# Two hybrid decoder layers on one core: S5 matmuls in a hand-written order, its U and y reordered through DRAM, layer 1's S5 operands made during layer 0's feed forward

## The chip, the core and the metric

One core of a Trainium2 chip runs the whole kernel in one launch: TensorE (matmul), VectorE, ScalarE, GpSimd, and SyncE, which issues most DMAs. The metric is the device time of one execution in microseconds, as a median of runs.

## The reference, cut to what matters

512 tokens, width 1024, two layers, all in float32. Each layer projects the tokens and mixes them in three branches, merges these with sigmoid gates, then an output projection, a layer norm, a feed forward of width 4096 and a second layer norm.

```python
u_pool, u_ssm, q, kv, g_nsa, g_merge = split(x @ w_in)
y_pool = pool_mixer(u_pool, ...)            # trailing means, grouped 128x128 matmul
# S5: 32 groups of 16 channels, 64 complex states each
h[t] = a * h[t-1] + Bbar @ u[t]             # associative scan over the 512 tokens
y = Re(C @ h) + d * u ; z = gelu(y) ; y_ssm = z * sigmoid(z @ w_glu + b_glu)
y_nsa = compressed / selected / window attention, gated
x = layer_norm(ALPHA * x + merged @ w_out)
x = layer_norm(ALPHA * x + relu(x @ w_ff1)**2 @ w_ff2)
```

In the compressed branch, keys and values of 32-token blocks pass through a two-layer MLP (`gelu(flat @ w1) @ w2`) before the attention.

## The kernel before, in words

Every large product is float32 as three fp32r matmuls (high x high, high x low, low x high), `mm3_`, lines 93 to 102. It is a generator: one step is three matmuls. Weights come through `wload` (line 70): SyncE loads 512 KB into one of two staging buffers `wst`, ScalarE casts it to `wh`, VectorE or GpSimd makes the rest `wl`, four buffers of each. `proj` is one 128-channel projection, 8 steps.

A planner orders each engine's instructions by priority and estimated time, except where `manual_schedule` keeps the written order. TensorE's order is written by hand in the attention part, where `run` takes a pattern string: a letter is a step of a named generator, a dot a step of `fill` (GLU, merge of the S5 branch, gates).

`s5_branch` (line 470) works in four rounds r of 8 groups. A round makes operands on GpSimd from the parameters (`step` and `cmul`, lines 450 to 455: Z, W, and the powers E by doubling), which ScalarE spreads into block form (525, 528). TensorE makes K (535) and transposes Z to lq (545), multiplies lq with U (551, the "q" product); VectorE and GpSimd rotate by E, scan along the chunks and rotate back into the state S (554 to 572); TensorE adds K x U and W x S into py (575, 577); a gelu follows. U (128 partitions, 4 tokens per chunk side by side) is made from the projection by 16 small ScalarE copies a round (465), and y is turned back by 16 more (582). In layer 0 rounds 2 and 3 take their E from VectorE; in layer 1 all of it is on GpSimd.

In a layer the branches are called one after the other: pooling (four projections, each followed by its 128x128 product), S5, the merge of the pooling branch, `nsa_early` (values, gate, two key projections); the planner interleaves them. Then follows `nsa_branch`: query projections, the compressed branch (lines 710 to 720: 32 float32 matmuls a layer with 65 columns, each recorded twice; its weights w in two buffers), and the attention.

`feed_forward` runs 8 chunks of up and down. In layer 0 its last chunk is woven with the next layer's U projection (`norm_xw`), then GpSimd applies the layer norm's gain and bias (`ln_affine`), and the residual goes to DRAM (`xd`, line 1148).

Of the kernel before, what the change touches and what calls it, by code (L numbers as in the profile page):

```python
# [9 lines left out]
F32 = mybir.dt.float32  # L10
R = mybir.dt.float32r
# [15 lines left out]
class Kern:  # L27
# [41 lines left out]
    def wload(self, ap, pool=None):  # L69

        n = ap.shape[1]
        with ExitStack() as order:
# [6 lines left out]
            self.nc.sync.dma_start(st, ap)  # L79
# [135 lines left out]
    def ln_affine(self, rs, g, b):  # L215

        gl = self.nc.gpsimd
        with self.tc.manual_schedule(engines={mybir.EngineType.Pool}):
            for r in (rs[3], rs[0], rs[1], rs[2]):
                for h in range(2):  # L220
                    s = slice(h * 512, (h + 1) * 512)
                    gl.tensor_tensor(r[:, s], r[:, s], g[:, s], OP.mult)  # L222
                    gl.tensor_tensor(r[:, s], r[:, s], b[:, s], OP.add)
# [81 lines left out]
    def pool_branch(self, i, pb):  # L305
        nc = self.nc
        nxt = self.proj(i, 4)
        wh, wl = self.wload(self.A["wpool"][i])
        for g in range(4):
            ps = nxt  # L310
            w = 2 << g
            u, *a = [self.t(pb, [128, 528], F32, "e", 6) for k in range(2 if g == 0 else 3)]
            for q in (u, *a):
                nc.vector.memset(q[:, 0:16], 0.0)
            nc.scalar.copy(u[:, 16:], ps)
            s, d = u, 1
            while d < w:
                nc.vector.tensor_tensor(a[0][:, 16:], s[:, 16:], s[:, 16 - d:528 - d], OP.add)
                s, a, d = a[0], a[::-1], 2 * d
            nc.vector.tensor_tensor(s[:, 16:32], s[:, 16:32], self.pfix[:, g, :], OP.mult)  # L320
            zf = s[:, 16:]
            nc.vector.scalar_tensor_tensor(zf, zf, 1.0 / w, u[:, 16:], op0=OP.mult, op1=OP.subtract)
            zh = self.t(pb, [128, 512], R, "e", 6)
            zl = self.t(pb, [128, 512], R, "e", 6)
            self.hi_lo(zh, zl, zf)
            if g < 3:
                nxt = self.proj(i, 5 + g)
            p2 = self.psum("o")
            c = slice(g * 128, (g + 1) * 128)
            self.mm3(p2, [((wh[:, c], wl[:, c]), (zh, zl))])  # L330
# [4 lines left out]
            self.y_pool.append((yh, yl))  # L335

# [119 lines left out]

    def s5_inputs(self, pss):

        self.U = []
        for pu in pss:  # L460
            u = self.t(self.hp, [128, 512], R, "hi_b").bitcast(F32).rearrange("p (g c) -> p g c", g=4)
            for g in range(4):
# [6 lines left out]
    def s5_branch(self, i):  # L469
        nc, v, tc = self.nc, self.nc.vector, self.tc  # L470
        gl = nc.gpsimd
        are, aim, are2, aim2, kre, kim, dec = self.s5a
        pr, pi = self.s5ph
        zt = []
        with tc.tile_pool(name=f"s5{i}", bufs=1, reuse_waits="tile") as sp:
            T = lambda shape, dt, tag, bufs=1: self.t(sp, shape, dt, tag, bufs)
            U = self.U
            for r in range(4):
                u = U[r]
                gs = slice(i * 16 + 4 * r, i * 16 + 4 * r + 4)  # L480
                col = lambda q, n: q[:, gs].unsqueeze(1).unsqueeze(3).to_broadcast([128, 2, 4, n])
                dd = T([32, 4, 32], F32, "dd")
                nc.sync.dma_start(dd, self.A["ddiag"][i, :, 4 * r:4 * r + 4])
                bc = T([128, 4, 64], F32, "bc", 2)
                nc.sync.dma_start(bc, self.A["s5bc"][i, :, :, r * 64:(r + 1) * 64])

                Zc = T([128, 2, 4, 64], F32, "Zc")
                Wc = T([128, 2, 4, 80], F32, "Wc")

                def step(y, x, ar, ai):  # L490
                    n = x.shape[3]
# [755 lines left out]
```

## Time and profile before

| | |
|---|---|
| median of 3 runs | 1804.28 us (1802.28 to 1805.58) |
| the profiled execution | 1810.14 us |
| its span, first to last instruction | 1808.4 us |
| TensorE busy in it | 1694.7 us, 94% |
| mean granted TensorE clock | 0.976 of 2.4 GHz |
| VectorE, ScalarE, GpSimd busy | 1142.7, 795.7, 514.2 us |
| DMA | 161.67 MB, 89 GB/s over the span |

The profile is of one execution; times in it are microseconds from its first instruction. An engine's busy time includes what an instruction waits inside; "idle" is time between its instructions, and the profile names what released the next one. A granted clock between 0.5 and 1 is the mean of a stretch at 1.2 and at 2.4 GHz.

### The profile page before, as it was taken

What the parts mean: (1) busy time and instruction counts of PE and PEld (TensorE: products, weight loads), DVE (VectorE), ACT (ScalarE), POOL (GpSimd) and SP (SyncE); (2) the same over time, 40 slices, a digit from 0 to 9 for tenths busy, and PEclk for the clock granted to TensorE, in tenths of its full rate; (3) what the DMA queues carried; (4) which work ended last, traced back from release to release, by engine and by line L of the source; (5) the groups of instructions that cost most, each with busy time, mean ns of one, the idle gap of its engine ahead of it and who ended that gap; (6) DMA issues with size and microseconds to landing.
All of it is one profiled execution on the core that took longest, in us unless ns stands there. A gap on an engine that the chain in (4) does not pass through costs nothing.

```text
span 1808.4 us, 22625 instructions
## 1 busy us (share of the span) xinstructions
PE 1694.7 (94%) x8356; PEld 1409.7 (78%) x8356; DVE 1142.7 (63%) x2161; ACT 795.7 (44%) x1517; POOL 514.2 (28%) x612
## 2 busy tenths in 40 slices
PE   3989889999999999999998889999999999999996
PEld 2877777778779888888896777777787888888885
DVE  8786667776578645444566555776766684444447
ACT  2645545656534333223264456465564342223321
POOL 3966421321023202000059995122212060000002
PEclk9999999999999999999999999899999999999998
DMA  5221151111251334232222212311124233222231
GB/s 189 76 82 44 43 172 49 57 59 59 82 176 38 121 104 145 94 104 95 76 78 83 83 53 69 128 59 57 61 61 141 91 105 105 93 94 93 94 103 61
DMA packets 51375, 161.67 MB, mean 89 GB/s; under 512 B 10816, under 2 KB 11584, under 8 KB 51264
## 3 DMA queue, kind: packets, MB, share of 16 engines
q1 hardware_dynamic: 48960, 154.85, 25.9%
q10 hardware_dynamic: 2304, 5.37, 0.9%
q8 instruction: 65, 1.06, 0.2%
q14 instruction: 46, 0.38, 0.1%
HBM read 153.92 MB, written 6.29 MB: 89 GB/s over the span
## 4 chain that ended last, share of the span: by engine, by line
PE 65%; DVE 15%; POOL 8%; ACT 6%; issue 3%; DMA 2%; ACTq 0%; SPq 0%; DVEq 0%; POOLq 0%
PE mm L98 12%; PE mm L99 12%; PE mm L100 12%; PE s L99 4%; PE s L100 4%; PE s L98 4%; PE t L100 3%; PE t L98 3%; PE t L99 3%; ACT st L582 3%; PE o L749 2%; PE t L848 2%; DVE wl L85 1%; POOL wl L85 1%; ACT wh L82 1%
## 5 line engine op out<-in xcount | busy, mean ns | idle before, releaser
L82 ACT CAST wh<-wst 128x1024 fp32r<-128x1024 f32 (+1 forms) x260 | 269.9, 1041 | 450.9 <-PE s L100 217.0
L98 PE MATMUL mm<-xh,wh 128*128 128x512 f32 (+1 forms) x1088 | 432.3, 397 | 6.1 <-ACT hi_b L465 3.1
L85 DVE TENSOR_TENSOR wl<-wst,wh 128x1024 fp32r<-128x1024 f32 (+1 forms) x202 | 269.1, 1333 | 252.1 <-ACT wh L82 251.7
L100 PE MATMUL mm<-xh,wl 128*128 128x512 f32 (+1 forms) x1088 | 423.9, 390 | 0.0
L99 PE MATMUL mm<-xl,wh 128*128 128x512 f32 (+1 forms) x1088 | 423.7, 389 | 0.0
L98 PEld LDWEIGHTS mm<-xh,wh 128*128 128x128 f32 x1088 | 208.1, 191 | 44.6 <-ACT hi_b L465 3.8
L100 PEld LDWEIGHTS mm<-xh,wl 128*128 128x128 f32 x1088 | 207.8, 191 | 42.2 <-issue 0.2
L99 PEld LDWEIGHTS mm<-xl,wh 128*128 128x128 f32 x1088 | 208.0, 191 | 35.4 <-issue 0.2
L85 POOL TENSOR_TENSOR wl<-wst,wh 128x1024 fp32r<-128x1024 f32 (+2 forms) x58 | 143.3, 2473 | 284.2 <-ACT wh L82 284.2
L222 POOL TENSOR_TENSOR xm<-xm,ln_g 128x512 f32<-128x512 f32 x24 | 43.9, 1830 | 357.4 <-PE t L238 357.4
L193 POOL TENSOR_TENSOR xm<-xm,ln_g 128x512 f32<-128x512 f32 x9 | 12.2, 1367 | 323.9 <-ACT xm L192 323.9
L821 ACT ACTIVATE P<-P,mx 128x512 f32<-128x512 f32 (+3 forms) x128 | 71.3, 559 | 69.8 <-DVE mx L819 69.2
L819 DVE CUSTOM_DVE_ANT_0 P<-s,mask 128x512 f32<-128x512 f32 (+3 forms) x128 | 59.4, 486 | 32.2 <-PE s L816 30.8
L62 DVE TENSOR_TENSOR Pl<-t,Ph 128x384 fp32r<-128x384 f32 (+1 forms) x96 | 57.2, 597 | 28.4 <-ACT Ph L61 28.4
L1034 DVE TENSOR_TENSOR xm<-xm,t 128x512 f32<-128x512 f32 x56 | 38.5, 688 | 55.3 <-PE t L100 54.5
L1034 DVE TENSOR_TENSOR xm<-xm,s 128x512 f32<-128x512 f32 x56 | 38.3, 684 | 44.0 <-PE s L100 44.0
L828 POOL TENSOR_SCALAR P<-P,sm,gate 128x128 f32<-128x128 f32 x32 | 14.5, 453 | 168.8 <-DVE sm L823 113.3
L1017 DVE TENSOR_TENSOR mt<-mt 128x512 f32<-128x512 f32 x64 | 55.9, 873 | 4.7 <-ACT mt L1016 4.7
L99 PE MATMUL mm<-lo_a,wh 128*128 128x512 f32 x128 | 52.4, 409 | 3.4 <-DVE lo_a L334 3.4
L61 ACT CAST Ph<-t 128x384 fp32r<-128x384 f32 (+1 forms) x96 | 48.4, 506 | 15.1 <-PE t L848 14.0
L98 PE MATMUL mm<-hi_a,wh 128*128 128x512 f32 x128 | 53.0, 416 | 0.2 <-ACT hi_a L333 0.2
L99 PE MATMUL s<-wl,hi_a 128*128 128x512 f32 x136 | 53.0, 390 | 0.0
(409 smaller groups left out, 3858.6 us busy)
## 6 DMA issues: line engine op xcount, KB each, us to landing
wst<-in_wf_dram SPq DMA_DIRECT2D x128, 512.0 KB, 3.5
wst<-in_win_dram SPq DMA_DIRECT2D x80, 512.0 KB, 3.2
wst<-in_wup_dram SPq DMA_DIRECT2D x24, 512.0 KB, 3.5
wst<-in_wout_dram SPq DMA_DIRECT2D x16, 512.0 KB, 4.2
xd<-xm SPq DMA_DIRECT2D x8, 512.0 KB, 4.1
w<-in_w_dram SPq DMA_DIRECT2D x8, 512.0 KB, 4.9
xm<-xd SPq DMA_DIRECT2D x8, 512.0 KB, 5.1
xm<-in_x_dram SPq DMA_DIRECT2D x4, 512.0 KB, 5.6
```

What stands on the lines that cost most here:

```text
L61: a = self.nc.scalar.copy(hi, src)
L62: b = self.nc.vector.tensor_tensor(lo, src, hi.bitcast(F32), OP.subtract)
L82: self.nc.scalar.copy(wh, st)
L85: e.tensor_tensor(wl, st, wh.bitcast(F32), OP.subtract)
L98: mm(out, ah, bh, start=first and i == 0, stop=False, **kw)
L99: mm(out, ah, bl, start=False, stop=False, **kw)
L100: mm(out, al, bh, start=False, stop=last and i == n - 1, **kw)
L582: nc.scalar.copy(dst[:, j], py[32 * j:32 * j + 32, g, :])
L819: v.tensor_tensor_reduce(out=p, in0=ss[qb], in1=self.mask[:, 384 - 128 * qb:512], scale=-1.0, scalar=3e38, op0=OP.add, op1=OP.min, accum_o ...
L821: nc.scalar.activation(p, p, AF.Exp, bias=mx[:, qb:qb + 1], scale=-1.0, accum_out=c)
L1017: v.tensor_tensor(h, h, h, OP.mult)
L1034: v.tensor_tensor(r, r, ps, OP.add)
```

## The change

- S5's TensorE order is written by hand. `first_branches` draws fill steps (pooling projections, `nsa_early`, the pooling's grouped products, its merge, in this order: 180 steps) between the pieces of the S5 generator `s5_`, which yields how many steps to put in. Round r is split in `front(r)` and `back(r)`.
- The pooling branch keeps its four results and does the grouped products after `nsa_early`.
- U and y: ScalarE copies the whole bank in one instruction, `across` writes it to DRAM and loads it back in four pieces in the other order.
- Operands Z, W and E of a round lie in one tile `zwe`, two of them. For layer 1 they are made by GpSimd alone in layer 0's feed forward (`s5_ahead`, one round per chunk from chunk 1), written to DRAM (`s5d`, 1.70 MB a round) and loaded from there by `s5_`.
- The gain and bias of layer 0's last layer norm are loaded at chunk 7, in halves, into the hidden-activation buffers; the residual's DRAM writes are issued after the first operand load of layer 1.
- Compressed branch: four weight buffers, loaded at its start; 66 columns for 65; both products before the evictions.
- The attention's pattern: the last step of the compressed softmax (the transposes of ec) stands after 15 dots, three score steps and two value steps, before after 11 dots; the product with it comes behind the first transposes.

```diff
+    def first_branches(self, i, pb):
+        def others():
+            yield from self.pool_(i, pb, res)
+            self.share = 2
+            yield from self.merge_(i, 0, self.y_pool)
+        res, n = [], 0
+        fill = others()
+        with self.tc.manual_schedule(engines={mybir.EngineType.PE}):
+            for k in self.s5_(i):
+                if i and k and self.late:
+                    for tb in range(4):
+                        self.nc.sync.dma_start(self.xd[tb], self.late[tb])
+                    self.late = None
+                for _ in range(k):
+                    n += next(fill, 1) is None
+            for _ in fill:
+                n += 1
+        return res[0]
...
+    def across(self, src):
+        d = self.t(self.dr, [4, 32, 4, 128], F32, "across", 8)
+        self.nc.sync.dma_start(d.rearrange("b x a c -> (b x) a c"), src)
+        def load(out):
+            for a in range(4):
+                self.nc.sync.dma_start(out[32 * a:32 * a + 32], d[:, :, a].rearrange("b x c -> x b c"))
+        return load
...
     def s5_inputs(self, pss):
         for pu in pss:
-            u = self.t(self.hp, [128, 512], R, "hi_b").bitcast(F32).rearrange("p (g c) -> p g c", g=4)
-            for g in range(4):
-                src = pu[32 * g:32 * g + 32].rearrange("p (c j) -> p j c", j=4)
-                for j in range(4):
-                    self.nc.scalar.copy(u[32 * j:32 * j + 32, g, :], src[:, j])
-            self.U.append(u)
+            q = self.t(self.hp, [128, 512], R, "lo_b").bitcast(F32).rearrange("p (j c) -> p j c", j=4)
+            self.nc.scalar.copy(q, pu.rearrange("p (c j) -> p j c", j=4))
+            self.U.append(self.across(q))
...
+    def s5_ahead(self, i, after):
+        with self.tc.tile_pool(name=f"s5a{i}", bufs=1, reuse_waits="tile") as pool:
+            qs = [self.t(pool, [128, 3328], F32, f"zwe{k}") for k in range(2)]
+            for r in range(5):
+                with self.tc.issue_after(after):
+                    if r < 2:
+                        self.nc.gpsimd.memset(qs[r][:, 0:2304], 0.0)
+                    if r < 4:
+                        self.s5_operands(pool, i, r, qs[r % 2], self.nc.gpsimd, True)
+                if r:
+                    with self.tc.issue_after(self.loaded):
+                        self.nc.sync.dma_start(self.s5d[r - 1], qs[(r - 1) % 2])
+                yield
...
+            def operands(r):
+                dd = T([32, 4, 32], F32, "dd")
+                nc.sync.dma_start(dd, self.A["ddiag"][i, :, 4 * r:4 * r + 4])
+                q = zwe[r % 2]
+                if i == 0:
+                    self.s5_operands(sp, i, r, q, v if r >= 2 else gl)
+                else:
+                    with tc.high_priority():
+                        nc.sync.dma_start(q, self.s5d[r])
+                return (dd, *self.s5_views(q))
...
+            def front(r):
+                dd, Z, W, EE = first if r == 0 else operands(r)
+                yield 3 if r else 10
...             # transposes of Z, lq copies, the matmuls of K
+                yield 3
...             # q products, rotation, K's copies, scans, the state S
+            def back(r):
...             # the matmuls of py, as before
+                q, y = st(), st()
+                nc.scalar.copy(q, py)
+                self.across(q)(y)
...             # gelu, as before
+            first = operands(0)
+            for r in range(4):
+                u = self.t(self.hp, [128, 512], R, "hi_b").bitcast(F32).rearrange("p (g c) -> p g c", g=4)
+                U[r](u)
+                U[r] = u
+            for r in range(4):
+                yield from front(r)
+                yield 26
+                back(r)
+                yield 10
...
-                            w = C([128, 1024], F32, "w1", 2)
-                            nc.sync.dma_start(w, self.A["w1"][i, kv, :, c * 1024:(c + 1) * 1024])
+                            w = ws1.pop(0)
-                                nc.tensor.matmul(hid[:, kv, 0:65], w[:, j * 128:(j + 1) * 128], src[kv][:, 8 * c + j:8 * c + j + 513:8],
+                                nc.tensor.matmul(hid[:, kv], w[:, j * 128:(j + 1) * 128], src[kv][:, 8 * c + j:8 * c + j + 521:8],
...
-        run("c.a.a..c..a...........c", c=compressed(0), a=scores(0))
+        run("c.a.a..c..a.....", c=c, a=scores(0))
-            p = "b..b..b..b..b.." if n == N - 1 else "a.a.b.b.a.b..b..bc."
+            p = "b..b..b..b..b.." if n == N - 1 else "a.a.b.b.a.b..b..bc." if n else "a.a.b.b.a......cb..b..b."
...
             nx = up(c + 1) if c < 7 else None
+            if c == 1 and i < DEPTH - 1:
+                ahead = self.s5_ahead(i + 1, self.affine.ins)
+            if 1 <= c < 7 and i < DEPTH - 1:
+                next(ahead, None)
+            if c == 7 and i < DEPTH - 1:
+                g, b = [], []
+                for q, tag, row in ((g, "hi_a", 4 + 4 * i), (b, "lo_a", 5 + 4 * i)):
+                    for h in range(2):
+                        q.append(self.t(self.hp, [128, 512], R, tag).bitcast(F32))
+                        nc.scalar.dma_start(q[h], A["ln"][row:row + 1, h * 512:(h + 1) * 512].to_broadcast([128, 512]))
```

## Rows read from the trace of the kernel before

**Rows 1.** The page: busy time by engine; shares of the chain that ended last.

```profile
PE 1694.7 (94%) x8356; PEld 1409.7 (78%) x8356; DVE 1142.7 (63%) x2161; ACT 795.7 (44%) x1517; POOL 514.2 (28%) x612
...
PE 65%; DVE 15%; POOL 8%; ACT 6%; issue 3%; DMA 2%; ACTq 0%; SPq 0%; DVEq 0%; POOLq 0%
```

**Rows 2.** Windows: length, busy of PE, PEld, DVE, ACT, POOL (instructions); clock, DMA share, GB/s.

```profile
74.00:235.00 161.00, 143.07 (x731) 119.30 (x732) 112.25 (x204) 83.16 (x178) 93.18 (x115) 0.93 0.19 63
235.00:288.00 53.00, 48.30 (x226) 41.55 (x224) 32.24 (x50) 20.85 (x42) 7.95 (x5) 0.87 0.40 136
600.00:900.00 300.00, 300.00 (x1325) 248.39 (x1325) 150.68 (x180) 92.64 (x114) 9.85 (x4) 1.00 0.33 107
945.00:1119.00 174.00, 153.83 (x791) 126.21 (x790) 101.22 (x151) 91.15 (x202) 158.51 (x258) 0.96 0.23 74
1119.00:1160.00 41.00, 37.26 (x175) 31.67 (x174) 24.78 (x44) 18.04 (x37) 6.22 (x5) 0.88 0.41 139
```

**Rows 3.** Waits of PE: who for whom, us in total, times, longest.

```profile
PE s L577 <- POOL Sr L569: 8.4, 4, 3.2
PE o L717 <- issue: 6.7, 2, 4.7
PE s L551 <- ACT lq L547: 5.5, 4, 2.3
PE t L793 <- DVE ec L789: 4.5, 2, 2.3
PE mm L98 <- ACT gate L643: 3.9, 2, 2.6
```

**Rows 4.** Timeline of DVE, layer 1's S5 round 1.

```profile
1024.45 0.69 DVE L554 TENSOR_TENSOR st<-s,E 128x512 f32<-128x512 f32 x1
...
1030.39 0.69 DVE L558 TENSOR_TENSOR st<-s,E 128x512 f32<-128x512 f32 x1 [1.51 <-POOL st L556]
1030.99 1.41 DVE L565 TENSOR_TENSOR_SCAN st<-s_dec,st 128x128 f32<-128x128 f32 x4
1033.79 3.62 DVE L565 TENSOR_TENSOR_SCAN st<-s_dec,st 128x128 f32<-128x128 f32 x4 [1.39 <-POOL st L559]
...
1039.49 0.69 DVE L571 TENSOR_TENSOR st<-st,E 128x512 f32<-128x512 f32 x1
```

**Rows 5.** Timeline of POOL, the same stretch.

```profile
1034.61 2.52 POOL L85 TENSOR_TENSOR wl<-wst,wh 128x1024 fp32r<-128x1024 f32 x1
...
1041.29 1.33 POOL L572 TENSOR_TENSOR Si<-st,st 128x508 f32<-128x508 f32 x1
```

**Rows 6.** Lines of ACT by form: busy us, mean ns, idle before.

```profile
L582 ACT COPY st<-s 32x128 f32<-32x128 f32 x128 | 48.5, 379 | 6.6 <-PE s L577 2.8 <-POOL E L455 2.3
L465 ACT COPY hi_b<-s 32x128 f32<-32x128 f32 x64 | 16.5, 257 | 3.3 <-PE s L100 2.5
L547 ACT COPY lq<-t 128x512 f32<-128x512 f32 x16 | 9.1, 585 | 2.5 <-PE t L545 2.3
```

**Rows 7.** Windows of L452 and L455 alone, layer 1's S5: length, DVE, POOL, clock.

```profile
945.00:1119.00 174.00, 0.00 (x0) 28.97 (x52) 0.96 0.23 74
...
945.00:1119.00 174.00, 0.00 (x0) 22.70 (x52) 0.96 0.23 74
```

**Rows 8.** DMA issues: count, KB each, median us to landing.

```profile
xd<-xm SPq DMA_DIRECT2D x8, 512.0 KB, 4.1
...
bc<-in_s5bc_dram SPq DMA_DIRECT2D x8, 128.0 KB, 3.3
```

**Rows 9.** Waits of SyncE's queue: us in total, times, longest.

```profile
SPq L79 <- DVE wl L85: 1028.5, 189, 37.5
```

**Rows 10.** Timeline of PE, compressed branch of layer 0: start, us, instruction, [idle before].

```profile
259.62 4.00 PE L717 MATMUL o<-src,w 128*128 128x65 f32 x32
268.31 7.06 PE L717 MATMUL o<-src,w 128*128 128x65 f32 x32 [4.70 <-issue]
```

**Rows 11.** Timeline of PE, eight 128-column float32 matmuls of S5.

```profile
1080.82 1.05 PE L551 MATMUL s<-hi_b,lq 128*128 128x128 f32 x8
```

More of the change, by code (lines that the diff above doesn't have):

```diff
@@ L302, in proj_, with pool_, grouped @@
         return ps
-    def pool_branch(self, i, pb):
+    def pool_(self, i, pb, early):
         nc = self.nc
-        nxt = self.proj(i, 4)
         wh, wl = self.wload(self.A["wpool"][i])
-        for g in range(4):
[L310 to L328, printed above, removed]
+        z = []
+        def grouped(g):
+            p2 = self.psum("mm")
             c = slice(g * 128, (g + 1) * 128)
-            self.mm3(p2, [((wh[:, c], wl[:, c]), (zh, zl))])
+            yield from self.mm3_(p2, [((wh[:, c], wl[:, c]), z[g])])
             yh, yl = self.pair("a")
@@ L482, in s5_branch @@
                 dd = T([32, 4, 32], F32, "dd")
                 nc.sync.dma_start(dd, self.A["ddiag"][i, :, 4 * r:4 * r + 4])
[L484 to L491, printed above, removed]
-                    tt = [T([128, 2, 4, 32], F32, f"ct{k}")[:, :, :, 0:n] for k in range(2)]
-                    self.cmul(gl, y, x, col(ar, n), col(ai, n), tt)
@@ L503, in s5_branch @@
-                EE = T([128, 2, 4, 128], F32, "E", 2)
-                E = [EE[:, 0], EE[:, 1]]
-                gl.memset(E[0][:, :, 0:1], 1.0)
-                gl.memset(E[1][:, :, 0:1], 0.0)
-                n, k = 1, 0
-                while n < 128:
-                    ee = [T([128, 2, 4, 64], F32, f"et{c}")[:, :, :, 0:n] for c in range(2)]
-                    self.cmul(v if i == 0 and r >= 2 else gl, EE[:, :, :, n:2 * n], EE[:, :, :, 0:n], col(pr[:, k], n), col(pi[:, k], n), ee)
-                    n, k = 2 * n, k + 1
@@ L547, in s5_branch @@
                     nc.scalar.copy(lq, pt)
+                    lqs.append(lq)
+                kp = self.psum("o")
+                for g in range(4):
+                    for c in range(2):
+                        zb = Z[c][:, g, 3].rearrange("p a x -> p (a x)")
+                        nc.tensor.matmul(kp[0:32, g * 128:(g + 1) * 128], zb, wf[c][:, g, 0:128], start=c == 0, stop=c == 1)
+                yield 3
+                q = []
+                for c in range(2):
                     q.append(self.psum("s", (128, 4, 128)))
@@ L646, in nsa_early @@
         for br in range(2):
-            ps = self.proj(i, 8 + br)
+            ps = yield from self.proj_(i, 8 + br)
             f = self.t(pb, [128, 512], F32, "e", 6)
@@ L1146, in feed_forward @@
             self.ln_affine(xs, g, b)
-            for tb in range(4):
-                nc.sync.dma_start(self.xd[tb], xs[tb])
+            self.late = xs
         else:
```

191 lines of the change are left out of this document (120 added, 71 removed).

## The prediction

> **What bounds the kernel now.** I read the page first: TensorE is busy 94% of the span and holds 65% of the chain that ended last, VectorE 15%, GpSimd 8%, ScalarE 6% [rows 1]. So the kernel is a queue of matmuls, and the question is where that queue has holes. The second view is busy time and granted clock by stage [rows 2]. In layer 0's feed forward (600 to 900 us) TensorE is busy 300.00 of 300 us at clock 1.00, 1325 matmuls, so one 512-column matmul costs 300/1325 = 0.226 us and a fill step of three costs 0.68 us: nothing is to be gained there. In the stage with the S5 branch it is busy 143.07 of 161 us at clock 0.93 (layer 0) and 153.83 of 174 us at 0.96 (layer 1); in the stage with the compressed branch 48.30 of 53 at 0.87 and 37.26 of 41 at 0.88. A granted clock of 0.93 is a mean of stretches at 2.4 and at 1.2 GHz; while it is at 1.2 a busy TensorE does half, so a stage loses (1 - clock) x its length besides its idle time. The third view, TensorE's waits over the span [rows 3], names the holes: the S5 state from GpSimd (8.4 us), the transposed operand lq from ScalarE (5.5), the gate's eviction (3.9), the compressed branch's weights (6.7), the compressed softmax ec (4.5).
>
> **What can be had at most.** Layer 0's S5 stage: 161 - 143.07 = 17.9 idle, 0.07 x 161 = 11.3 clock, 29.2 us. Layer 1's: 20.2 + 0.04 x 174 = 7.0, 27.1 us. Compressed branch, layer 0: 4.7 + 0.13 x 53 = 6.9, less 1.7, my estimate of idle time at 1.2 GHz that is counted twice, 9.9 us; layer 1: 3.7 + 0.12 x 41 = 4.9, less the same 1.7, 6.9 us. The ec wait 4.5 us. Sum 77.6 us.
>
> **Part 1, the S5 order by hand.** Now each of four rounds r has its matmuls placed by the planner; afterwards round r is: Z's transposes and K, 3 fill steps, the q matmuls, 26 fill steps, the y matmuls, 10 steps. What the order must cover is the chain from q to y. In layer 1, round 1, it now starts at 1024.45 and VectorE's part ends at 1039.49 + 0.69 [rows 4]; GpSimd's last sum ends at 1041.29 + 1.33 = 1042.6 [rows 5]: 18.2 us. In it VectorE waits 1.51 and 1.39 us for GpSimd [rows 4], and one scan group takes 3.62 us instead of 1.41 [rows 4] while GpSimd makes a wl for 2.52 us [rows 5]. Alone the chain is two products (1.38), a GpSimd sum (1.3), a product (0.69), a sum (1.3), four scans (1.41), four products (2.76), a sum (1.3): 10.1 us. With two wl of 1.3 and two merge products of 0.7 between, 14 us; that is the value I take, between 10.1 and 18.2, nearer the lower end because the operand work of part 2, which GpSimd now does between these sums, leaves layer 1. The cover: 26 steps of 0.68 are 17.7 us in rounds 2 and 3; in rounds 0 and 1, 7 and 9 of the steps are the value projections with 280 columns (by columns 0.37 us a step), so 15.5 and 14.9 us. Rounds 2 and 3 are covered, 0 and 1 barely. If a chain still takes 18.2, y is late by up to 3.3 us, and with the clock's share (11.3 us lost to it beside 17.9 idle in layer 0's stage, 0.63 per idle us) a round costs some 5. I charge two rounds: 10 us. The gate wait of 3.9 us stays [rows 3], since that eviction is not touched. The lq wait goes: lq's two copies (0.585 us each [rows 6]) get 3 fill steps and the K matmuls, 2.0 + 2.1 us, as cover.
>
> **Part 2, U and y through DRAM; operands made early.** 128 copies of 0.379 us for y and as many of 0.257 us for U (64 in the row, 64 more like it) leave ScalarE [rows 6], 81 us in all; 16 copies of about 0.59 us come, 9 us. ScalarE is not the bound, so the gain is only that lq, K and the casts stand behind less. In their place each round has a write of 256 KB and four loads of 64 KB, for U and for y: 80 DMAs on SyncE's queue. GpSimd's operand work in layer 1 is 106.1 us, four source lines of 22.70 to 30.96 us [rows 7], of its 158.51 us there [rows 2]; it moves into layer 0's feed forward, where GpSimd is busy 9.85 of 300 us [rows 2]. With eight copies that ScalarE did it is about 32 us a round against 192 matmuls = 43.5 us of feed-forward per call, so SyncE, which then writes 1.70 MB, finds it done. The nearest rows for a DRAM round trip are 4.1 us for a write and 3.3 for a load [rows 8], 7.4 us; the load waits in SyncE's queue for the write, and weight loads stand behind it. U's cover is 13 fill steps and Z's matmuls, 8.8 + 3 us: price 0, upper bound 7.4 a layer. y is read only by the GLU in the attention stage: 0. Layer 1's operands come back as 1.70 MB a round, by the 512 KB row between 4.1 and 3.25 x 4.1 = 13.3 us [rows 8]; their buffers are not those of the projection weights, so the load can begin before U is projected: 0, but 13.3 - 6.8 (ten steps) = 6.5 us once if it can't. Weights behind these transfers have slack: a weight load waits 1028.5/189 = 5.4 us on average for its staging buffer [rows 9], one of two, so it is a full weight period (24 x 0.226) ahead. The LN rows, now in four loads on ScalarE's queue, are needed only by GpSimd after the projection: 0. Layer 1's four residual writes of 512 KB move behind the first operand load on SyncE's queue and are read again only by the output projection: 0.
>
> **Part 3, compressed branch.** Now 32 matmuls take 4.00 us, then TensorE stands 4.70 us until the third weight tile is there, and the next 32 take 7.06 us at the lower clock [rows 10]; four buffers, loaded at the branch's start, remove that. I keep 1 us of 16.8. 66 columns for 65: 4.00/32 = 0.125 us now, eight 128-column float32 matmuls take 1.05 us, 0.131 each [rows 11], so column count hardly sets it: 128 matmuls, between -1.5 and +0.8 us; I take 0. The ec transposes get four more fill steps (2.7 us) and five attention steps ahead of them, against waits of at most 2.3 us [rows 3]: 4.5 us.
>
> **Sum.** S5 stages 56.3 - 13.9 = 42.4, compressed 15.8, ec 4.5: 62.7 us. From the profiled execution's 1810.1 that is 1747.4; the median of the runs is 5.9 us below it, so 1741.6. I say 1741.
>
> **A rule weighed.** The chain's slow scan is a VectorE instruction beside one long GpSimd instruction [rows 4, 5]. The Trainium skill (SBUF — State Buffer, "SBUF: two separate sides") says why: GpSimd and a VectorE instruction with two SBUF inputs take one port pair as an exclusive lock, and the loser blocks wholly. By that rule the operands moved into the feed forward would be paid there. The trace agrees with the blocking in this one place; whether it adds up to the whole of both engines' work is the third rival.
>
> **The rivals.** First, the chain stays as long as now. For: 18.2 us in a stage where layer 0's GpSimd work is unchanged. Against: layer 1's GpSimd is freed. All eight rounds late at 5 us, 40 instead of 10: 1771. Second, all holes close: only the gate wait stays, 10 us more than forecast: 1731; the whole 77.6 us would give 1727, with the lower bound of part 3 and the 3.6 us of measurement 1722. Third, GpSimd in the feed forward blocks VectorE: VectorE's 150.68/300 x 43.5 = 21.8 us and GpSimd's 32 per call are 53.8 in 43.5 us, 10.3 us late each for four calls, +41: 1782. Against: in layer 1's S5 stage the two sum to 259.7 busy us in 174 [rows 2], so they do run together, and VectorE's evictions read one SBUF operand. Fourth, on the other side: SyncE's queue. Every round trip holds it 7.4 us and weights come late; 16 trips all exposed are 118 us, less the 77.6: 1845. It turns slower than before from 77.6/16 = 4.9 us exposed per trip; against it stands the 5.4 us of staging slack. Fifth, it doesn't do what it says: only TensorE's order is by hand, the others' is planned, and an operand late by the plan stops the fills too; gain about nothing, 1804.
>
> **Chances.** Forecast 0.45 (its own range 1733 to 1755), chain as long 0.24, all holes 0.15, port 0.04, SyncE 0.08, nothing 0.04. Range 1720 to 1790: it takes in the first three rivals. Two versions closer than 0.2% (3.6 us) can't be told apart here. Faster 0.45 + 0.24 + 0.15 + 0.04 = 0.88, less 0.01 for two rivals at once; same 0.03; slower 0.08 + 0.02, the last from "nothing".
>
> **What would show it.** Right: TensorE idle under 8 us in each S5 stage with clock 0.98 or more, no wait at the third weight tile of the compressed branch, GpSimd under 60 us in layer 1's S5 stage. Part 1 wrong: y matmuls waiting for Sr or Si in most rounds. Part 2 wrong: TensorE waiting for wh behind SyncE, or feed forward below 100% busy. The prediction falls if q waits for U or Z comes late from DRAM in layer 1.

## The result and the profile after

The changed kernel takes 1783.99 us (median of 4 runs, 1780.6 to 1785.11) against 1804.23 (1802.28 to 1805.58) for the kernel before: ratio 0.9886, 95% interval 0.9868 to 0.9903. That is 20 us less where 63 were forecast. The page of the profiled execution, for [rows 1]:

```profile
span 1783.3 us, 22543 instructions
PE 1676.9 (94%) x8356; PEld 1402.0 (79%) x8356; DVE 1129.7 (63%) x2167; ACT 711.3 (40%) x1245; POOL 552.4 (31%) x640
```

TensorE's share, 94% in both kernels, says nothing new. To see where the time went, I cut both traces at the same places of the program: the end of the first norm's transposes, the first matmul of the compressed branch's hidden layer, the first score matmul, the next norm's first transpose, and the same in layer 1. Between two cuts both kernels run the same matmuls (the counts in brackets agree within a few). Columns are as in [rows 2]. The kernel before:

```profile
45.30:259.60 214.30, 196.17 (x1034) 165.85 (x1033) 148.46 (x294) 118.29 (x272) 126.18 (x186) 0.94 0.23 78
259.60:294.40 34.80, 30.10 (x146) 26.51 (x145) 23.77 (x38) 13.08 (x24) 4.75 (x2) 0.80 0.28 91
294.40:553.00 258.60, 249.35 (x1232) 200.91 (x1231) 181.18 (x423) 138.88 (x287) 50.90 (x37) 0.99 0.24 82
553.00:906.70 353.70, 353.41 (x1665) 296.76 (x1664) 197.04 (x264) 115.59 (x155) 37.85 (x20) 1.00 0.30 98
906.70:1138.30 231.60, 210.42 (x1142) 176.61 (x1141) 137.96 (x227) 130.42 (x299) 181.69 (x273) 0.97 0.25 83
1138.30:1171.20 32.90, 29.56 (x145) 25.70 (x144) 25.68 (x44) 13.01 (x24) 4.90 (x2) 0.84 0.29 96
1171.20:1433.10 261.90, 252.06 (x1231) 203.36 (x1230) 181.44 (x423) 138.93 (x287) 50.43 (x37) 0.98 0.25 81
```

and the changed kernel:

```profile
45.40:257.40 212.00, 190.65 (x1035) 164.23 (x1034) 152.55 (x299) 82.72 (x152) 125.77 (x184) 0.94 0.32 104
257.40:282.90 25.50, 25.50 (x146) 22.43 (x146) 20.86 (x34) 13.00 (x24) 4.78 (x2) 1.00 0.25 83
282.90:541.00 258.10, 251.23 (x1232) 202.16 (x1231) 175.86 (x422) 138.93 (x287) 52.66 (x37) 0.99 0.25 82
541.00:905.70 364.70, 355.81 (x1666) 298.13 (x1665) 199.91 (x264) 115.11 (x155) 173.32 (x274) 0.99 0.36 115
905.70:1125.10 219.40, 204.32 (x1141) 177.06 (x1140) 135.51 (x239) 82.44 (x146) 78.32 (x49) 0.97 0.42 140
1125.10:1150.60 25.50, 25.50 (x146) 22.43 (x145) 20.89 (x34) 13.01 (x24) 4.77 (x2) 1.00 0.27 83
1150.60:1408.20 257.60, 250.01 (x1232) 201.25 (x1231) 175.87 (x422) 138.92 (x287) 52.71 (x37) 0.99 0.25 82
```

Read the second number, the length. Layer 0's S5 stage went from 214.3 to 212.0 us (-2.3), layer 1's from 231.6 to 219.4 (-12.2), the compressed branch by -9.3 and -7.4, the attention by -0.5 and -4.3, and layer 0's feed forward became 11.0 us longer. The sum is -25.0 us, and the spans differ by 25.1. The medians differ by only 20.2 us: the profiled execution of the kernel before lies 5.9 us above its median, that of the changed kernel 1.1. Some 5 of the 25 us so belong to that one execution, and a change of 2 or 3 us in a stage is not told from chance. TensorE's waits for the whole span, for [rows 3], say what it stands on:

```profile
PE mm L98 <- ACT wh L82: 12.8, 6, 3.8
PE mm L99 <- DVE wl L85: 9.0, 5, 5.2
PE t L98 <- ACT wh L82: 8.9, 1, 8.9
PE t L589 <- DMA zwe<-s5d: 5.9, 1, 5.9
PE mm L100 <- DVE wl L85: 5.7, 2, 4.4
PE s L640 <- POOL Si L631: 3.4, 1, 3.4
PE t L929 <- DVE P L913: 2.7, 2, 1.4
...
PE o L834 <- ACT pch L61: 1.9, 2, 1.0
PE o L834 <- DVE pcl L62: 1.8, 2, 0.9
```

The waits of [rows 3] for Sr, lq and the compressed branch's w are gone, and the one for the gate is down from 3.9 to 0.3 us; one for Si of 3.4 us is left. In their place TensorE waits for weights, the high half `wh` or the low half `wl`: under `mm` 12.8 + 9.0 + 5.7 = 27.5 us (18.6 of them in layer 0's S5 stage, 4.4 in layer 1's), against 2.6 in the kernel before:

```profile
PE mm L98 <- ACT wh L82: 1.6, 2, 1.2
PE mm L99 <- DVE wl L85: 1.0, 2, 0.5
```

In layer 0 this is VectorE's timeline (start, length, instruction) at the first such stop:

```profile
83.41 3.04 DVE L85 TENSOR_TENSOR wl<-wst,wh 128x840 fp32r<-128x840 f32 x1 [3.68 <-ACT wh L82]
86.97 2.50 DVE L624 TENSOR_TENSOR_SCAN st<-s_dec,st 128x128 f32<-128x128 f32 x4
89.39 1.55 DVE L337 TENSOR_TENSOR e<-e 128x512 f32<-128x512 f32 x2
90.87 2.38 DVE L624 TENSOR_TENSOR_SCAN st<-s_dec,st 128x128 f32<-128x128 f32 x4
94.53 1.02 DVE L85 TENSOR_TENSOR wl<-wst,wh 128x840 fp32r<-128x840 f32 x1
102.58 0.93 DVE L85 TENSOR_TENSOR wl<-wst,wh 128x560 fp32r<-128x560 f32 x1
```

The second and the third low half come 11 and 19 us after the first; in between stand round 0's scans and the pooling sums. From 84 to 155 us VectorE is nearly full, in the kernel before it was not (columns as above; the kernel before, then the changed one):

```profile
84.00:155.00 71.00, 66.15 (x332) 54.35 (x332) 55.45 (x99) 37.03 (x68) 49.44 (x64) 0.95 0.18 64
84.00:155.00 71.00, 49.65 (x269) 42.73 (x268) 67.47 (x140) 28.69 (x65) 54.22 (x75) 0.82 0.21 63
```

The three low halves above belong to the value weights of `nsa_early`. In the kernel before they came at 179 to 197 us, and GpSimd made two of them:

```profile
179.03 2.45 POOL L85 TENSOR_TENSOR wl<-wst,wh 128x840 fp32r<-128x840 f32 x1
```

The line `self.share = 2`, which gives GpSimd every second low half, stands ahead of `nsa_early` in the kernel before and behind it in the changed one. So VectorE makes 20 low halves in layer 0's S5 stage, before 16. The list of the change doesn't name this, and the prediction has no term for it.

In the feed forward these are TensorE, GpSimd and SyncE's queue, one fence each:

```profile
691.33 0.79 PE L98 MATMUL t<-wh,hi_a 128*128 128x512 f32 x1 [8.88 <-ACT wh L82]
```

```profile
676.24 1.01 POOL L524 TENSOR_SCALAR zwe<-Wc 64x320 f32<-64x320 f32 x1
677.53 4.75 POOL L85 TENSOR_TENSOR wl<-wst,wh 128x1024 fp32r<-128x1024 f32 x2
684.39 2.35 POOL L85 TENSOR_TENSOR wl<-wst,wh 128x1024 fp32r<-128x1024 f32 x1 [0.27 <-ACT wh L82]
688.02 2.84 POOL L85 TENSOR_TENSOR wl<-wst,wh 128x1024 fp32r<-128x1024 f32 x1
```

```profile
662.92 19.72 SPq L79 DMA_DIRECT2D wst<-in_win_dram  x4
686.76 4.45 SPq L79 DMA_DIRECT2D wst<-in_wf_dram  x2
```

GpSimd also makes the low halves of layer 1's first four weight tiles, and had done so all along (`wload` with a pool of its own). Now they stand behind the S5 operands on it; both staging buffers stay held, SyncE issues the four loads over 19.7 us, and the feed forward's own weights (`wf`) stand behind those.

### The profile page after: what moved, and what is told of

Read it like the earlier page. It is cut to its first block, busy times and chain, and to the rows that moved or that the text cites. A ratio compares the mean times of both kernels' runs of the same rounds, so it can differ in the third digit from the quotient of the medians.

```text
span 1783.3 us, 22543 instructions
## 1 busy us (share of the span) xinstructions
PE 1676.9 (94%) x8356; PEld 1402.0 (79%) x8356; DVE 1129.7 (63%) x2167; ACT 711.3 (40%) x1245; POOL 552.4 (31%) x640
## 4 chain that ended last, share of the span: by engine, by line
PE 71%; DVE 12%; POOL 10%; DMA 3%; ACT 2%; issue 1%; SPq 0%; DVEq 0%; ACTq 0%; POOLq 0%
PE mm L98 15%; PE mm L99 14%; PE mm L100 14%; PE s L99 3%; PE s L98 3%; PE s L100 3%; PE o L834 3%; PE t L98 2%; PE t L99 2%; PE t L100 2%; PE t L929 2%; DVE wl L85 1%; PE s L901 1%; ACT wh L82 1%; POOL ct L461 1%
## 5 line engine op out<-in xcount | busy, mean ns | idle before, releaser
L85 DVE TENSOR_TENSOR wl<-wst,wh 128x1024 fp32r<-128x1024 f32 (+2 forms) x208 | 276.7, 1332 | 251.6 <-ACT wh L82 251.3
L100 PE MATMUL mm<-xh,wl 128*128 128x512 f32 (+1 forms) x1088 | 419.3, 385 | 5.7 <-DVE wl L85 5.7
L99 PE MATMUL mm<-xl,wh 128*128 128x512 f32 (+1 forms) x1088 | 418.8, 385 | 0.0
L100 PEld LDWEIGHTS mm<-xh,wl 128*128 128x128 f32 x1088 | 205.1, 188 | 48.2 <-DVE wl L85 6.8
L85 POOL TENSOR_TENSOR wl<-wst,wh 128x1024 fp32r<-128x1024 f32 x52 | 132.1, 2543 | 243.1 <-ACT wh L82 243.0
L193 POOL TENSOR_TENSOR xm<-xm,ln_g 128x512 f32<-128x512 f32 x9 | 12.2, 1367 | 321.4 <-ACT xm L192 321.4
L906 ACT ACTIVATE P<-P,mx 128x512 f32<-128x512 f32 (+3 forms) x128 | 71.3, 558 | 62.7 <-DVE mx L904 62.3
L222 POOL TENSOR_TENSOR xm<-xm,hi_a 128x512 f32<-128x512 f32 x8 | 12.6, 1581 | 182.7 <-PE t L238 182.7
L222 POOL TENSOR_TENSOR xm<-xm,ln_g 128x512 f32<-128x512 f32 x16 | 30.1, 1884 | 121.8 <-PE t L238 121.8
L98 PE MATMUL t<-wh,hi_a 128*128 128x512 f32 x128 | 50.7, 396 | 8.9 <-ACT wh L82 8.9
```

The source lines that it names most:

```text
L85: e.tensor_tensor(wl, st, wh.bitcast(F32), OP.subtract)
L98: mm(out, ah, bh, start=first and i == 0, stop=False, **kw)
L99: mm(out, ah, bl, start=False, stop=False, **kw)
L100: mm(out, al, bh, start=False, stop=last and i == n - 1, **kw)
L906: nc.scalar.activation(p, p, AF.Exp, bias=mx[:, qb:qb + 1], scale=-1.0, accum_out=c)
```

## The experiments

Theory: the S5 chain is covered as forecast, but the engines beside TensorE have more to do than its strict order allows, and what comes late is weights, in three places: layer 0's S5 stage, the feed forward, the start of layer 1's. Rivals: SyncE's queue with its DRAM trips; the chain. The times are medians; a stage length is from one profiled execution, cut as above. Intervals are about 0.2% to each side, so differences of 3 us or less between two kernels are not told apart. The runs are from several chips, on which the kernel before took 1802.5 to 1805.1 us; taken by the ratios, a difference between two of the kernels comes out up to 3.5 us other than by the medians.

**w0_vector: the four low halves on VectorE.**

```diff
-w0 = [self.wload(A["win"][i + 1, j], w0p) for j in range(4)]
+w0 = [self.wload(A["win"][i + 1, j], w0p, self.nc.vector) for j in range(4)]
...
```

The part left out lets `wload` take the engine as an argument.

> The changed kernel, with the low parts of layer 1's first four weight tiles (made in layer 0's feed forward) taken from GpSimd to VectorE. Theory: in the changed kernel these four stand on GpSimd behind layer 1's S5 operands, hold both staging buffers from 666 to 691 us, and so keep SyncE from loading the up weights; TensorE then waits 8.9 us and, with the clock, loses 11. Without it the stretch 670 to 700 us is full and the time is 1773 us (1770 to 1776). Rival, SyncE's queue is late because of the DRAM writes of the operands: the hole stays, 1784 us. Second rival, the hole only moves to the next tile that VectorE makes late: 1780 to 1784.

1770.73 us, ratio 0.9821 (0.98 to 0.9841): 13 less than the changed kernel (12 by the ratios). The feed forward is 353.5 us, as before. The stretch that held the hole (columns as above):

```profile
670.00:700.00 30.00, 30.00 (x134) 24.86 (x133) 19.63 (x22) 11.46 (x14) 29.57 (x57) 1.00 0.58 174
```

TensorE is full, at clock 1.00, while GpSimd is busy nearly throughout. So the operand work costs nothing there; the low halves queued behind it did. The third rival's price is out: TensorE loses nothing, and the stage is as long as before. Its mechanism is not out. GpSimd's 29.57 us hold time that its instructions wait inside: a copy of one form takes 0.39 us alone and 1.39 when it begins during a low half on VectorE.

```profile
671.33 1.40 DVE L85 TENSOR_TENSOR wl<-wst,wh 128x1024 fp32r<-128x1024 f32 x1 [0.70 <-ACT wh L82]
671.60 1.39 POOL L521 COPY zwe<-Zc 64x256 f32<-64x256 f32 x1
679.62 0.39 POOL L521 COPY zwe<-Zc 64x256 f32<-64x256 f32 x1
```

By the Trainium skill (SBUF — State Buffer, "SBUF: two separate sides") the two exclude each other only where both need the shared port pair; these rows, where the copy ends 0.26 us after the low half, agree.

**part3_alone: the compressed branch and the attention order on the kernel before.** The edit is these two parts of the diff.

> The kernel before, with the change's compressed branch (66 columns, four weight buffers loaded at its start) and its new attention order alone. By the prediction's Part 3: 15.8 us less and 4.5 us less, 1784 us, which is all that the whole change gave; the S5 rebuild then gave nothing. By the trace of the changed kernel, where the hidden layer's stage is full and the wait for ec has come back at pch, pcl and P: 9 to 16 us less, 1788 to 1795 us.

1795.46 us, ratio 0.9958 (0.994 to 0.9975): 7 less. Layer 0's compressed stage falls to 25.4 us as in the changed kernel; layer 1's stays 32.9, with TensorE busy all of it at clock 0.74, behind a wait of 2.7 us for the rope (VectorE). In the changed kernel, behind the rebuilt S5 stage, that wait is absent and the stage gains in both layers.

This run is also a second look at the S5 code of the kernel before. Layer 0's S5 stage:

```profile
45.30:254.40 209.10, 192.18 (x1034) 162.83 (x1033) 146.24 (x292) 118.40 (x272) 126.50 (x187) 0.97 0.26 85
```

That is 209.1 us where the profiled execution of the kernel before shows 214.3 and the changed kernel 212.0. So the traces show no gain of the S5 rebuild in layer 0; its gain is in layer 1 (234.1 us here, 219.4 in the changed kernel).

**copies: U and y by ScalarE again.** The two `across` trips out, the 16 copies a round of the kernel before in.

> The changed kernel, with S5's inputs and outputs reordered by ScalarE copies of 32 partitions, as in the kernel before, in place of the trips through DRAM; all else as changed. Rival, the trips cost time by their latency and by filling SyncE's queue (11.9 us for eight loads in layer 1): 1770 to 1779 us without them. Theory, weights made late are the loss and the trips are beside it: ScalarE has 128 more small copies a layer, and its casts come later still, 1784 to 1800 us.

1794.88 us, ratio 0.9956 (0.9941 to 0.9971): 11 more than the changed kernel, 9.0 of it in layer 0's S5 stage (221.0 us). The trips through DRAM pay, and the queue rival falls. Where it hurts is the pooling products' eviction, queued on ScalarE and VectorE: TensorE waits 12.0 us for its low half `lo_a`, and 5.5 us for lq.

**inplace1: layer 1's operands in layer 1.**

```diff
-                if i == 0:
-                    self.s5_operands(sp, i, r, q, v if r >= 2 else gl)
-                else:
-                    with tc.high_priority():
-                        nc.sync.dma_start(q, self.s5d[r])
+                self.s5_operands(sp, i, r, q, v if i == 0 and r >= 2 else gl)
...
-            if c == 1 and i < DEPTH - 1:
-                ahead = self.s5_ahead(i + 1, self.affine.ins)
-            if 1 <= c < 7 and i < DEPTH - 1:
-                next(ahead, None)
```

> The changed kernel without the operands made ahead: GpSimd, VectorE and ScalarE make layer 1's S5 operands in layer 1's S5 stage, as in layer 0, and nothing of them goes through DRAM. In the feed forward GpSimd is then free for the four weight tiles, so the hole at 682 to 691 us goes as in w0_vector (11 to 13 us less), and so does the 6 us stop for the operands' load. The prediction's Part 2 prices the work in the stage at 2.4 to 6.5 us a round; by the theory that weights come late when the three engines are full, layer 1's S5 stage then loses as much as layer 0's, 25 to 30 us in place of 18: 1775 to 1790 us. Rival, making them ahead gained nothing: 1762 to 1770 us.

1799.67 us, ratio 0.9975 (0.9961 to 0.999). The feed forward is 353.5 us again, and layer 1's S5 stage 247.9, 28.5 more than with operands made ahead; the time is above the theory's range. Against w0_vector, which has no hole in the feed forward either, it is 28.9 us more. (The price of 2.4 to 6.5 us a round that the expectation takes from Part 2 does not stand there.) TensorE stands at round 0's operands:

```profile
PE t L585 <- ACT zwe L521: 15.4, 1, 15.4
PE o L594 <- ACT zwe L526: 6.8, 2, 6.4
```

**order_alone: both of the last two.** Of the S5 rebuild only the order by hand is left.

> The changed kernel with ScalarE's copies in place of the DRAM trips, and layer 1's operands made in its S5 stage: of the S5 rebuild only TensorE's order by hand is left, with the round kept in two halves (and the new compressed branch). The prediction's Part 1 said that this order closes most holes by itself: about 10 us of 56 left, which would be 1755 to 1765 us. Theory, a strict order that runs while weights and operands come late stops TensorE for each of them: the copies cost 11 us and the operands in place 29 in the other runs, so 1800 to 1815 us, above part3_alone (1795), where the planner ordered TensorE.

1814.01 us, ratio 1.0049 (1.0033 to 1.0065): 9 us slower than before, and by the medians 18.6 us slower than part3_alone (16 by the ratios). It differs from part3_alone by that order and the halved round, and also by the grouped pooling products behind `nsa_early`, the low halves of `nsa_early`'s weights on VectorE alone, and S5's buffers; the loss is that of all these together. Layer 1's S5 stage (231.6 us before, 234.1 in part3_alone) takes 253.3:

```profile
900.40:1153.70 253.30, 209.68 (x1141) 180.37 (x1140) 144.97 (x241) 130.43 (x299) 175.55 (x271) 0.92 0.24 80
```

Forecast and theory are far apart here, and the theory holds. Its reason, that the planner could give TensorE other work while operands were late and a fixed order can't, fits the waits (16.0 us for round 0's zwe alone) but is not shown apart from the other differences.

**operands_left_out: layer 0's operands of rounds 1 to 3 not made**, on w0_vector.

```diff
-                q = zwe[r % 2]
+                q = zwe[r % 2 if i else 0]
                 if i == 0:
-                    self.s5_operands(sp, i, r, q, v if r >= 2 else gl)
+                    if r == 0:
+                        self.s5_operands(sp, i, r, q, gl)
...
```

> w0_vector (1770.7 us) with the S5 operands of layer 0's rounds 1 to 3 left out (all four rounds use round 0's): GpSimd's some 65 us of small products in 80 to 200 us, VectorE's E of rounds 2 and 3, ScalarE's copies into zwe. Theory: what makes layer 0's weights late in 80 to 155 us (28 us lost there) is that these operands run beside the chain and the pooling sums, on GpSimd beside VectorE too (the low part took 3.04 us beside it and 1.02 without); at least half of the 28 us goes, 1750 to 1757 us. Rival, VectorE's own pooling sums and chain are enough to make them late: less than 6 us go, 1765 to 1771 us.

1751.11 us, ratio 0.9693 (0.9666 to 0.972): 19.6 less than w0_vector by the medians, 23 by the ratios. In the traces layer 0's S5 stage is 20.0 us shorter. The stage, and the stretch in which VectorE was nearly full:

```profile
46.00:237.40 191.40, 184.82 (x1035) 159.81 (x1035) 129.07 (x243) 73.33 (x128) 68.01 (x75) 0.99 0.35 114
84.00:155.00 71.00, 64.42 (x376) 55.64 (x375) 51.74 (x94) 31.27 (x63) 16.71 (x11) 0.98 0.27 87
```

191.4 us at clock 0.99, with the chain, the sums and all weights as they were; VectorE is busy 51.74 of the 71 us, in w0_vector 66.96.

**sums_left_out: one addition per pooling tile**, on w0_vector (`while d < w` becomes `while d < 2`).

> w0_vector with one addition in each pooling tile in place of one, two, three and four (the six others of each layer are left out, some 7 us of VectorE a layer). Theory, VectorE is the engine that is late at 84 to 112 us, and each us taken from it there comes back at the next weight tile: 4 to 8 us less in layer 0 and 0 to 3 in layer 1, 1760 to 1766 us. Rival, the operands beside it set the pace: 1768 to 1771 us.

1763.78 us, ratio 0.9765 (0.9737 to 0.9793): 7 less (10 by the ratios), with layer 0's stage at 205.1 us (6.3 less) and layer 1's at 215.4 (3.1 less). The stages are from the fastest of its four executions (1759.9 us; two took 1767). In it, some 7 us taken from VectorE in a layer come back nearly in full in layer 0 and by half in layer 1. So not the operands alone but other work on VectorE counts.

**Buffers.** pool_bufs6 takes the pooling tiles `e` from the layer's pool of six; wpool_own (on w0_vector) also gives the pooling's second weight tiles of its own.

> The changed kernel, with the pooling sums in the six buffers e of the layer's pool (as in the kernel before) in place of three of their own. Theory: with three, ScalarE's copies of the next pooling tile wait 6.4 and 3.5 us for a buffer, and the weight casts behind them come late; with six the loss of 30 us in 80 to 155 us falls to 15 to 22, and the time is 1770 to 1777 us. Rival, VectorE itself has too much to do in 83 to 104 us (its instructions stand close there): the casts come earlier but the low parts don't, 1782 to 1786 us.

1782.84 us, ratio 0.9889 (0.9861 to 0.9918): no change. My theory of three buffers was wrong, the rival right.

> w0_vector (1770.7 us; TensorE loses 28 us in layer 0 between 80 and 155 us) with the pooling branch's second weight in tiles of its own in S5's pool, so that it holds none of the four weight tiles, and the pooling sums in the layer's six buffers e. Theory A, tiles: in layer 0 the key weights (cast at 124.9, loaded by 103) wait for a tile, because the pooling weight and the three value chunks hold all four; with one more, the stops of 3.3 and 4.4 us at 126 to 132 us go, 1761 to 1765 us. Theory B, VectorE: its instructions stand without a gap from 84 to 138 us and the low parts are late whichever tile they write; the stops move or shrink by less than 3 us, 1768 to 1771 us.

1767.46 us, ratio 0.9794 (0.9772 to 0.9817): 3.3 less than w0_vector, between the two theories, and not in layer 0 (214.0 against 211.4 us) but in layer 1 (214.7 against 218.5). The longest single stop in the S5 stages is now for the key's eviction, 6.0 us. In layer 0's stage TensorE's waits for weights are down from 16.9 us to 3.8, and the stage is no shorter, since waits for that eviction and for Si (5.0 us) stand in their place. A tile more moved the stop. Neither buffers nor late weights as such are the cause in layer 0; late weights are how it shows.

**Order of the filling work** (on w0_vector). values_first puts `nsa_early` ahead of the pooling; spread makes pooling tiles 0 and 1, then the values, then tiles 2 and 3, then the keys.

> w0_vector with the order of TensorE's filling work turned round: first the value and key products of the attention (their weights), then the pooling products and sums. Theory B, VectorE's load of pooling sums on top of round 0's S5 chain at 84 to 112 us makes the value and key weights late: they are then made before the chain begins, and of the 28 us lost in 80 to 155 us 10 to 20 go, 1751 to 1761 us. Theory A (four weight tiles, one held by the pooling weight) also gains here, the two stops at 126 to 132 us only, 1761 to 1765 us. If neither decides, the same load on VectorE comes later and stops other weights: 1768 to 1775 us.

> w0_vector with the pooling products in two halves: two tiles, then the value products, then the two tiles with the longer sums, then the keys. Theory: the jam on VectorE (pooling sums on top of round 0's chain, 84 to 112 us) is thinned, and the two stops for value weights at 94 to 102 us go, but the sums then stand in front of other tiles: 1760 to 1768 us. Rival, the load is only moved, as in values_first: 1770 to 1780 us.

1785.06 us, ratio 0.9896 (0.987 to 0.9922), and 1768.6, ratio 0.98 (0.9774 to 0.9826). values_first loses 14 us, outside all three of its ranges, with y now waiting for Sr and Si and the pooling products for their operands; spread is not told apart from w0_vector.

**Order of the rounds** (on w0_vector). late0 in layer 0 alone; late_both in both layers, and with zwe_split. The edit of late0 (in late_both without `if i == 0`):

```diff
-                yield 3 if r else 10
+                yield 3 if r else 36 if i == 0 else 10
...
-                yield 26
+                yield 20 if i == 0 else 26
...
-                yield 10
+                yield 8 if i == 0 else 10
```

> w0_vector (1770.7 us) with layer 0's four S5 rounds begun later in TensorE's order: 36 pieces of filling work ahead of the first in place of 10, and 34 from round to round in place of 42. Theory 1, a clash in time: S5's chain of round 0, the pooling sums and the value weights meet on VectorE and GpSimd at 84 to 140 us, while both have room from 155 to 280 us; moved apart, 8 to 15 of the 28 us go, 1756 to 1763 us. Theory 2, a sum of work: the stops move with the rounds, and closer rounds (34 pieces are some 23 us, as long as the chain from q to y) add waits for Sr and Si: 1769 to 1776 us.

> late0 in both layers, with the load of the operands in three parts as in zwe_split. In layer 1 the first transposes then come some 18 us later than now: the stop of 6.6 us for zwe goes, and of the 18 us lost in layer 1's S5 stage 6 to 10 go by theory 1, 1748 to 1757 us; by theory 2 the wait for Si (2.4 to 3.5 us now) grows in each round, 1765 to 1775 us.

1777.86 us, ratio 0.9847 (0.9823 to 0.987), and 1790.96, ratio 0.9922 (0.9893 to 0.9951): 7 and 20 more than w0_vector, 2 and 16 above the ranges of theory 2. In late_both TensorE waits

```profile
PE s L644 <- POOL Sr L632: 10.2, 3, 5.4
...
PE s L644 <- POOL Si L635: 7.8, 5, 2.6
```

and besides 10.0 us for `lo_a` and 8.8 for the gate. later_both, as late_both with 60 steps ahead of the first round and 16 between q and y, was expected at 1755 to 1775 us and 5 to 15 above late_both. It took 1792.76 us, ratio 0.9939 (0.992 to 0.9957): not told apart from late_both, with 12.9 us of waits for Sr and 7.9 for Si.

Theory 1's gain did not come in any of the three. The direction is that of theory 2, a sum of work; but the edits move the rounds and close them up at once, so a clash isn't excluded by itself. With 20 steps in place of 26 between q and y the sums are late, so the prediction's cover of some 15 to 18 us was needed and nearly enough.

**zwe_split: the first operand load in three parts** (on w0_vector), the second round's not beside it.

```diff
-                    with tc.high_priority():
-                        nc.sync.dma_start(q, self.s5d[r])
+                    if r == 0:
+                        with tc.high_priority():
+                            for s in (slice(0, 1024), slice(1024, 2304), slice(2304, 3328)):
+                                nc.sync.dma_start(q[:, s], self.s5d[r, :, s])
+                    else:
+                        nc.sync.dma_start(q, self.s5d[r])
```

> w0_vector with layer 1's first load of S5 operands from DRAM in three parts (Z, W, E: 512, 640 and 512 KB in place of 1664), and the second round's load no longer issued beside it. Theory: TensorE's stop of 6.6 us at 933 to 940 us is the landing of both loads of 1664 KB (8.4 us and more) at over 370 GB/s; Z alone lands in some 3 us, the stop shrinks to 1 to 3 us, and the time is 1765 to 1768 us. Rival, the transfers are issued as late as before, behind U's writes in SyncE's queue, and that sets the landing: the stop stays above 5 us, 1769 to 1772 us.

1770.0 us, ratio 0.9813 (0.9786 to 0.9839): no change in the time, though the stop halved from 6.6 to 3.3 us; the one for Si grew from 2.2 to 3.4.

**best and best_share1.** best is w0_vector, wpool_own and zwe_split together; best_share1 also gives GpSimd every second low half in layer 1's S5 stage.

> w0_vector, wpool_own and zwe_split together: layer 1's first weights on VectorE in the feed forward, the pooling weight in tiles of its own, the operands' first load in three parts. The sums of what they gave one by one (13.3, 3.3 and 0.7 us) is 1766.7 us; if the time that zwe_split gave back in a wait for Si is free of it once the weights come earlier, 1762 to 1765 us.

> As best, and in layer 1's S5 stage GpSimd makes every second low part (five of ten), as it does in the stages behind. There it is busy 50 of 145 us. By the sum of work (theory 2) VectorE is late in layer 1, and moving 5 us of its work lets weights and chain come earlier: 3 to 6 us less than best. Rival, GpSimd's part of the chain (Sr, Si) then stands behind the low parts: 0 to 5 us more than best.

1763.55 us (1761.21 to 1763.86), ratio 0.9767 (0.9745 to 0.9789), and 1766.13, ratio 0.9792 (0.9769 to 0.9816). best beats both kernels, by 41 and 20 us. Its S5 stage of layer 0, its feed forward and its S5 stage of layer 1:

```profile
45.40:259.50 214.10, 195.11 (x1035) 168.33 (x1034) 156.11 (x300) 81.96 (x151) 130.34 (x188) 0.94 0.31 100
540.20:893.70 353.50, 353.49 (x1665) 296.80 (x1664) 202.34 (x268) 114.97 (x155) 169.48 (x270) 1.00 0.37 119
893.70:1103.80 210.10, 202.04 (x1141) 174.81 (x1140) 138.50 (x240) 82.21 (x146) 76.10 (x49) 0.98 0.43 146
```

In layer 0 nothing is gained, though TensorE waits there only 1.6 us for weights: it waits for Si (5.8), the key's eviction (4.6) and lq (4.5) instead. best_share1 gains nothing: layer 1's S5 stage is 214.4 us, and the rival's bound (0 to 5 more) holds. So giving GpSimd a share of the low halves in layer 1 again doesn't help; in layer 0 that was not tried.

## Why the prediction was wrong

The forecast was 62.7 us off the profiled execution; 25.1 came (20.2 by the medians). By its steps:

- **Compressed branch: right.** 15.8 us forecast, 16.7 measured (9.3 and 7.4), and no wait at the third tile. That layer 1's half did not come without the S5 change ahead of it (part3_alone) was not seen.
- **Attention: the sum right, the way not.** 4.5 us forecast, 4.8 measured (0.5 and 4.3). The wait for ec is gone; new ones for P, pch and pcl stand there, 6.4 us in sum, while one for Pl, which the prediction doesn't name, fell from 6.7 to 2.4. The sum is in part luck: layer 0's stage takes 255.3 us in best and 261.2 in pool_bufs6, with the same attention code.
- **Part 1, the chain: right, but not the bound.** y waits for Si once, 3.4 us, where two late rounds were charged, and not for Sr; layer 1's GpSimd is busy 50.51 us from 940 to 1085 us. The first rival fell. The gate wait, kept at 3.9 us, went as well. But the prediction's own sign of being right, TensorE idle under 8 us in each S5 stage at clock 0.98 or more, did not come: it is idle 21.4 us at 0.94 and 15.1 at 0.97.
- **Part 2, "Weights behind these transfers have slack: 5.4 us", and with it a price of 0: the step that failed.** The slack was a mean wait of SyncE for a staging buffer, and [rows 9] name what it waits for: VectorE's low half. They show the load ahead of VectorE, not the weight ahead of TensorE. With the order by hand, round 0's chain, the pooling sums and the value weights' low halves, which are now all on VectorE, come together from 84 to 155 us. VectorE is busy 67.47 of the 71 us there (55.45 before), and TensorE's waits for weights go from 2.6 us in the whole span to 27.5. In layer 0 the forecast's stage is 214.3 - (29.2 - 7) = 192 us; measured 212.0, 20 us short. Leaving out three rounds of operands takes 20.0 us off w0_vector's stage, to 191.4; that this is the forecast's length is chance, since the forecast kept that work. The prediction asked only whether the chain, lq and the loads are late; the work beside them on VectorE and GpSimd, for the most part in the kernel before as well, it put at nothing. sums_left_out shows VectorE's part of it, and wpool_own and best that weights made earlier only let another wait take their place.
- **Part 2, operands in the feed forward at 0: wrong, by 11.0 us** in the trace, 13 in the medians. GpSimd's own time was sized well: 173.32 - 37.85 = 135 us, 34 a round where 32 were worked out. The step failed on what else stands in GpSimd's order: four low halves with two staging buffers behind them. That stage's [rows 2] row, GpSimd 9.85 us, held them and was read as room only.
- **Part 2, the operand load: its upper bound came true.** 5.9 us stopped where 0 was taken and 6.5 given as the bound. Halving the stop (zwe_split) gave no time back.

The sum of what failed: 20 in layer 0, 11 in the feed forward, 8 in layer 1 (forecast 211.5 us, measured 219.4; best reaches 210.1), 39 us; gap 62.7 - 25.1 = 37.6, the rest being what the compressed branch and the attention gave beyond the forecast. Of the rivals, the fifth had the right mechanism (an operand late by the plan stops the fills too) and the wrong price. On GpSimd in the feed forward the third had the right engine for a wrong reason; its 1782 us is near by chance. The blocking that it names is seen in w0_vector's rows, but TensorE lost nothing by it. The fourth fell with copies.

What is shown: the feed forward's hole (one edit closes it); that operands made in place cost 20 us in layer 0 (three of its four rounds) and some 29 in layer 1; that the order by hand, without the DRAM trips and the operands made ahead, loses. Open: which part of layer 0's operand work (GpSimd's share of the chain, VectorE's E in rounds 2 and 3, ScalarE's copies) is the 20 us, as they were left out together; and what the low halves moved from GpSimd to VectorE cost in layer 0.

## What to carry to other kernels

A slack is slack against the engine that the wait names, and only in the order in which it was measured: for each engine, list what stands in its order in the stage as it will be, and ask which of it the bottleneck needs. A strict order on the busiest engine did not pay here while operands came late; the operands made ahead were worth more than the order. Before giving an idle engine new work, look for the few instructions it already has there and what they hold (here two staging buffers, and with them SyncE's queue).

## What was not expected of the hardware

One low half of 840 columns took 3.04 us on VectorE while GpSimd worked on layer 0's operands, and the same form 1.02 us 11 us later, also beside GpSimd (the expectation of operands_left_out says without it). Beside the first, seven GpSimd instructions ran one behind the other at 0.29 to 0.40 us each, and the eighth took 1.08. The second began 0.15 us ahead of GpSimd's sum Sr, and this time the sum took long: 1.99 us, where the same form took 1.33 in [rows 5]. Loads of 1664 KB issued in pairs at layer 1's start took 10.2 us to landing (median of two), among weight, residual and U transfers.
